# Softmax division moved from the probabilities to the gate of an attention block, by way of a row through DRAM

## Chip, core and metric

The program runs on one core of one Trainium2 chip. The metric is the device time of one execution in microseconds; the kernel before took 1666.42 us, the median of three runs between 1665.95 and 1667.75 us. Engines are named as in the profile: PE (matmuls), PEld (its weight loads), DVE, ACT, POOL, and SP, which only issues DMAs.

## What is computed

The reference is one layer: one input projection, two groups of mixers beside each other (sparse attention and a state-space scan), gates, one output projection and a LayerNorm. The attention's core, for each query block of 128 rows:

```python
s = jnp.einsum('bqgrd,bqkgd->bqgrk', qg, kg).astype(jnp.float32) * scale
s = jnp.where(valid[:, :, None, None, :], s, -jnp.inf)
p = jax.nn.softmax(s, axis=-1).astype(vg.dtype)
o = jnp.einsum('bqgrk,bqkgd->bqgrd', p, vg)
...
o_attn = _dsa_attention(q, k, v, q_idx, k_idx, w_idx) * jax.nn.silu(z_attn)
```

There are 1024 rows of 2048 columns, 8 query heads in 2 groups (4 heads share a key head), head width 128, and each query keeps 256 keys. The selection is a mask that is added to the scores, so the kernel works with whole rows of keys.

## The kernel before

Rows are handled in two halves of 512 (h = 0, 1). PE works through one long stream of matmuls: projection pieces (names `pj`, with x and w each split in a rounded high part `xh`, `wh` and a rest `xl`, `wl`, three matmuls for one product), and at the end the output projection, whose seven block products need what the mixers wrote to the DRAM tensors `mx` (`mx1_0` to `mx1_7` are the attention of the second half: two heads of a pair are two of these tensors). Weights come by DMA into `wr`, ACT rounds them to `wh`, DVE or POOL forms `wl`.

Everything else is written as Python generators (`t_attn`, `t_split`, `t_ssd` and more) that run beside the stream. A planner (`Flow`) steps a generator when its inputs, buffers and engines are free by the planner's own clock, and a second pass (`Queue.order`) puts the recorded calls in the order in which each engine gets them. Each engine then takes its instructions strictly in that order, and waits where an input is late. So a change to one task moves the order of nearly all that follows. For elementwise work that DVE or POOL may do, `Flow.pick` (L671) chooses by the same clocks.

The attention of one half and one key head (`t_attn`, L1852) is eight blocks: query blocks i, each as two pairs of heads pr. Three lanes take the blocks in turn. For one block:

- queries are loaded and split, PE makes the scores of the two heads in PSUM tiles `a`, `t_rowmax` (L1950) adds the mask, scales and takes the row maximum into the tile `pt`, which has (i+1)*128 columns;
- ACT takes the exponential in place and sums each row into `sm` (L1899), DVE the reciprocal of the two sums (L1901);
- POOL multiplies both `pt` tiles in place by their reciprocal (L1904, `gscale` L752);
- for each of the i+1 key blocks PE transposes a 128x128 piece of each head, `t_split` (L1958) rounds it on ACT and forms the rest on DVE, and PE multiplies by v into the PSUM tile `o`, where rows are the head's columns and columns are the queries (L1929 to L1931);
- DVE multiplies `o` by the gate (L1938), which was loaded as [128, 2, 128] from `z`, and two DMAs write the result to `mx` (L1943).

Of the kernel before, what the change touches and what calls it, by code (L numbers as in the profile page):

```python
# [13 lines left out]
ALU = mybir.AluOpType  # L14
# [4 lines left out]
P = 128  # L19
# [749 lines left out]
class Layer:  # L769
# [669 lines left out]
    def start_tasks(self):  # L1439
        fl = self.fl  # L1440
        fl.add(self.t_tables(0), 1, "rot", ROTS)
        self.ev_k = [Event(), Event()]
        self.ev_w = [Event(), Event()]
        self.ev_dt = [Event(), Event()]
        self.ev_row = [Event(), Event()]
        self.kk, self.score, self.nlog = {}, {}, [0, 0]
        self.ev_score = [Event(), Event()]
        self.ev_mask = {i: Event() for i in range(8)}
        self.m_sc = {i: self.scratch(f"mask{i}", [P, (i + 1) * P], BF) for i in range(2, 8)}
        self.ev_mask[0].cells = self.ev_mask[1].cells = [[0.0]]  # L1450
        self.mixed = [[self.scratch(f"mx{h}_{e}", [P, HALF]) for e in range(16)] for h in range(2)]
        self.hst = [self.scratch(f"hst{g}", [P, 256]) for g in range(4)]
        self.arow = [self.scratch(f"arow{h}", [64, P]) for h in range(2)]
        self.q_sc = [[self.scratch(f"q{h}_{g}", [4, P, HALF]) for g in range(2)] for h in range(2)]
        self.z_sc = [[self.scratch(f"z{h}_{g}", [4, P, HALF]) for g in range(2)] for h in range(2)]
        self.k_sc = [[self.scratch(f"k{h}_{g}", [P, HALF]) for g in range(2)] for h in range(2)]
        self.v_sc = [[self.scratch(f"v{h}_{g}", [P, HALF]) for g in range(2)] for h in range(2)]
        self.h_sc = [[[self.scratch(f"h{h}{s}_{d}", [P, HALF]) for d in range(4)] for s in range(4)] for h in range(2)]
        self.y_sc = {m: [self.scratch(f"y{m}_{k}", [P, HALF]) for k in range(8)] for m in (7, 6)}
        self.ev_y = {m: [Event() for _ in range(8)] for m in (7, 6)}  # L1460
        self.halves, self.left = [], {}
        self.ev_join = {(c, st): Event() for c in range(2) for st in range(4)}
        self.sums, self.ev_sum = {}, {(m, c, st): Event() for m in OUT for c in range(2) for st in range(4)}
        self.ev_kv = {(h, g, x): Event() for h in range(2) for g in range(2) for x in "kv"}
        self.ev_q = {(h, n): Event() for h in range(2) for n in range(8)}
        self.ev_z = {(h, n): Event() for h in range(2) for n in range(8)}
        self.ev_mix = {}
        for h in range(2):
            for e in range(16):
                self.ev_mix[h, e] = [Event() for _ in range(2 if e >= 8 else 4)]  # L1470
        self.ssd_n, self.ev_part = {}, {}
        self.p_sc = [[[self.scratch(f"pt{h}_{g}_{j}", [P, 2, HALF]) for j in range(3)] for g in range(4)] for h in range(2)]
        self.x_sc = {m: [self.scratch(f"x{m}_{k}", [P, HALF]) for k in range(8)] for m in (1, 2, 3, 4)}
        self.ev_x = {m: [Event() for _ in range(8)] for m in (1, 2, 3, 4)}
        self.stash, self.stt, self.prod, self.taken, self.backs = {}, {}, {}, set(), {}
        self.ev_h = {(h, g): Event() for h in range(2) for g in range(4)}
        self.tab = {}
        self.lnev = [Event() for _ in range(8)]
        self.ev_gain = Event()
        self.ev_rows = [Event() for _ in range(4)]  # L1480
        self.ev_res = {(prod, h, dc + c): Event() for prod, (h, dc) in self.ROWS.items() for c in range(2)}
        for k in range(8):
            src = [self.a["xt"][h, 8 * kh + k] for kh in range(2) for h in range(2)]
            fl.add(self.t_forms(src, {m: self.x_sc[m][k] for m in self.x_sc}, {m: self.ev_x[m][k] for m in self.x_sc}), 3, f"form_{k}", 100e3)
        self.o_sc = {m: [[self.scratch(f"o{m}_{c}_{k}", [P, 512]) for k in range(8)] for c in range(2)] for m in (1, 2, 3, 4)}
        for c in range(2):
            for k in range(8):
                src = [self.wo_at(n, c, k) for n in (11, 12, 21, 22)]
                fl.add(self.t_wforms(src, {m: self.o_sc[m][c][k] for m in self.o_sc}), 6, f"wform_{c}{k}", WFORMS + (8 * c + k) * WSTEP)
        for i in range(8):  # L1490
            fl.add(self.t_bias(i), 6, f"bias{i}", BIAS + i * WSTEP)
        for h in range(2):
            for blocks in ((2,), (3,)) if h == 0 else ((4, 7), (5, 6)):
                fl.add(self.t_topk(h, blocks), 3, f"topk{h}")
            for g in range(2):
                self.start_attention(h, g)
# [355 lines left out]
    def t_attn(self, h, g, st, todo):  # L1852
        fl, nc = self.fl, self.nc
        while todo:
            i, pr = todo.pop(0)
            n = (i + 1) * P
# [6 lines left out]
            pt = [fl.new("s4" if h else "u", [P, 1024 if h else 512]) for _ in heads]  # L1863
# [13 lines left out]
            sm = fl.new("sm", [P, 16])  # L1877
# [21 lines left out]
                fl.act(pt[r][:, 0:n], pt[r][:, 0:n], AF.Exp, bias=sm[:, 4 + r:5 + r], accum_out=sm[:, 6 + r:7 + r])  # L1899
            yield Need("V")  # L1900
            nc.vector.reciprocal(sm[:, 8:10], sm[:, 6:8])  # L1901
            yield Need("G")
            for r in range(2):
                fl.gscale(pt[r][:, 0:n], pt[r][:, 0:n], sm[:, 8 + r:9 + r])  # L1904
            fl.free(sm)
            yield Need("P", o=1, u=2)
            o = fl.new("o", [P, 256])
            gate = fl.new("u", [P, 2, P])
            fl.dma(gate, src(self.z_sc))
            spare = [fl.new("u", [P, 512], R)]  # L1910
            nk = i + 1
            ahead, kb = [], 0
            while kb < nk or ahead:
# [19 lines left out]
                if len(spare) > 1 and (len(spare) + len(ahead) > 3 or kb == nk):  # L1933
                    fl.free(spare.pop())
            fl.free(*spare, *pt)
            yield Need("V")
            g2 = gate.rearrange("p r s -> p (r s)")
            fl.tt("V", g2, o, g2, ALU.mult)  # L1938
# [2 lines left out]
            for r in range(2):  # L1941
                e = 4 * g + heads[r]
                fl.dma(self.mixed[h][e][:, q0:q0 + P], gate[:, r])  # L1943
                fl.signal(self.ev_mix[h, e][i - 4 * h])
            fl.free(gate)
            st["lanes"] += 1
            if st["lanes"] == 8:
                fl.signal(self.ev_att(h, g))
# [456 lines left out]
```

## Time and profile before

| what | value |
|---|---|
| median of three runs | 1666.42 us (1665.95 to 1667.75) |
| the profiled execution | 1665.7 us, span of its instructions 1663.9 us |
| PE busy | 1604.7 us, 96% of the span |
| DVE, ACT, POOL busy | 1345.0, 987.3, 271.9 us |
| DMA | 431.67 MB, mean 259 GB/s |

Busy time is a union of spans whose ends are modelled for PE: a matmul of 512 columns shows as about 0.39 us, but the next starts 0.227 us later. The granted clock is 1.00 from 52 us up to the last stretch. The work of the attention lies in four stretches, by its scaling instructions on POOL: 244 to 314 us, 756 to 861 us, 926 to 1045 us and 1134 to 1276 us.

### The profile page before, as it was taken

The page shows a single profiled execution, that of the slowest core. Times are in us where ns is not written, and L with a number is a line of the kernel's source. Part 1 is how long each engine was busy: PE and PEld are TensorE (multiplying, and loading weights), DVE is VectorE, ACT ScalarE, POOL GpSimd, SP SyncE. Part 2 cuts the span into 40 slices and gives each one's busy share as a digit, 9 for nine tenths or more (in the row PEclk, how much of TensorE's full clock was granted, in tenths as well). Part 3 has the DMA queues.
Part 4 walks back from the last instruction along what each step waited for, and adds up shares of the span by engine and source line. Part 5 has one row for each costly group of instructions (what it writes and reads, how often), then busy time and mean ns, then how long its engine had stood idle before and what let it go on. Part 6 is the DMA issues. An engine that isn't in the chain of part 4 may idle for free.

```text
span 1663.9 us, 26382 instructions
## 1 busy us (share of the span) xinstructions
PE 1604.7 (96%) x7989; PEld 1339.3 (80%) x7989; DVE 1345.0 (81%) x2991; ACT 987.3 (59%) x1920; POOL 271.9 (16%) x321
## 2 busy tenths in 40 slices
PE   7999999999999999999999999999999899999993
PEld 6888888888887888787788888888888788888782
DVE  7887655568899988898965777899986888988966
ACT  6657867565575599998832455657655444333431
POOL 3200022111114100101320322113111001000212
PEclk8999999999999999999999999999999999999997
DMA  9579998695477799999989886996766998878997
GB/s 311 167 243 366 299 254 233 205 315 153 133 206 232 226 303 300 302 276 296 334 272 340 266 280 195 290 297 208 229 206 191 301 337 260 270 238 297 336 231 177
DMA packets 272686, 431.67 MB, mean 259 GB/s; under 512 B 29600, under 2 KB 87328, under 8 KB 272032
## 3 DMA queue, kind: packets, MB, share of 16 engines
q1 hardware_dynamic: 259872, 406.93, 74.0%
q0 software_dynamic: 12672, 23.07, 9.3%
q8 instruction: 62, 1.02, 0.3%
q14 instruction: 80, 0.66, 0.1%
HBM read 338.56 MB, written 131.17 MB: 282 GB/s over the span
## 4 chain that ended last, share of the span: by engine, by line
PE 83%; DVE 8%; DMA 3%; issue 3%; ACT 1%; POOL 1%; SPq 0%; POOLq 0%; DVEq 0%; ACTq 0%
PE pj L467 64%; PE a L467 11%; PE o L467 8%; DVE u L467 3%; DMA wr<-wt 2%; DVE wl L467 1%; DVE wr L467 1%; DVE xl L467 1%; ACT u L467 1%; DVE s L467 1%; DMA u<-xn 1%; DVE sm L467 1%; ACT wh L467 0%; DMA u<-xt 0%; DMA u<-mx 0%
## 5 line engine op out<-in xcount | busy, mean ns | idle before, releaser
L467 PE MATMUL pj<-xh,wh 128*128 128x512 f32 (+1 forms) x1520 | 591.0, 389 | 7.5 <-ACT wh L467 4.2
L467 PE MATMUL pj<-xh,wl 128*128 128x512 f32 (+1 forms) x1520 | 582.6, 384 | 7.1 <-DVE wl L467 7.1
L467 PE MATMUL pj<-xl,wh 128*128 128x512 f32 (+1 forms) x1520 | 581.8, 383 | 0.2
L467 ACT ACTIVATE wh<-wr 128x512 fp32r<-128x512 f32 (+1 forms) x488 | 304.0, 626 | 400.3 <-PE pj L467 201.2
L467 DVE TENSOR_TENSOR wl<-wr,wh 128x512 fp32r<-128x512 f32 (+1 forms) x456 | 316.8, 700 | 117.1 <-ACT wh L467 112.7
L467 PEld LDWEIGHTS pj<-xh,wl 128*128 128x128 f32 x1520 | 287.5, 189 | 64.5 <-DVE wl L467 9.4
L467 PEld LDWEIGHTS pj<-xh,wh 128*128 128x128 f32 x1520 | 287.6, 189 | 60.6 <-ACT wh L467 5.6
L467 PEld LDWEIGHTS pj<-xl,wh 128*128 128x128 f32 x1520 | 287.7, 189 | 49.8 <-POOL xl L467 0.3
L467 PE MATMUL a<-u,u 128*128 128x512 f32 (+3 forms) x776 | 176.6, 344 | 3.3 <-DVE u L467 1.6
L467 DVE TENSOR_TENSOR u<-u,u 128x512 f32<-128x512 f32 (+7 forms) x240 | 150.6, 636 | 9.6 <-ACT u L467 7.7
L467 PEld LDWEIGHTS a<-u,u 128*128 128x128 f32 x776 | 129.8, 189 | 28.8 <-DVE s L467 5.4
L467 ACT ACTIVATE u<-u 128x512 f32<-128x512 f32 (+4 forms) x209 | 118.5, 576 | 55.7 <-DVE u L467 46.3
L467 ACT ACTIVATE u<-s,sm 128x1024 bf16<-128x1024 f32 (+7 forms) x132 | 128.8, 977 | 8.3 <-DVE sm L467 4.9
L467 PE MATMUL pj<-wh,xh 128*128 128x512 f32 x310 | 125.4, 404 | 2.5 <-DVE u L467 1.5
L467 PE MATMUL pj<-wh,xl 128*128 128x512 f32 x310 | 121.1, 392 | 1.5 <-DVE xl L467 1.5
L467 PE MATMUL pj<-wl,xh 128*128 128x512 f32 x310 | 120.9, 390 | 0.0
L467 ACT ACTIVATE xh<-u 128x512 fp32r<-128x512 f32 (+1 forms) x184 | 102.1, 585 | 29.5 <-DVE u L467 16.1
L467 DVE TENSOR_TENSOR wr<-wr,wr 128x512 f32<-128x512 f32 x160 | 115.4, 725 | 3.1 <-DMA wr<-wt 2.8
L467 DVE TENSOR_TENSOR xl<-u,xh 128x512 fp32r<-128x512 f32 (+1 forms) x168 | 113.0, 697 | 4.4 <-ACT xh L467 3.8
L467 ACT ACTIVATE a<-a 128x512 f32<-128x512 f32 (+3 forms) x160 | 77.2, 504 | 44.2 <-PE a L467 42.0
L467 POOL DMA_DIRECT2D o<-wo x64 | 53.8, 865 | 292.8 <-DMA o<-wo 137.3
L467 ACT ACTIVATE u<-a 128x256 fp32r<-128x256 f32 (+3 forms) x182 | 61.5, 363 | 63.8 <-PE a L467 58.8
(164 smaller groups left out, 2076.8 us busy)
## 6 DMA issues: line engine op xcount, KB each, us to landing
wr<-wt SPq DMA_DIRECT2D x424, 256.0 KB, 4.6
u<-xt SPq DMA_DIRECT2D x80, 256.0 KB, 5.5
u<-mx SPq DMA_DIRECT2D x72, 256.0 KB, 4.9
o<-wo POOLq DMA_DIRECT2D x64, 256.0 KB, 6.7
u<-x SPq DMA_DIRECT2D x64, 256.0 KB, 5.2
wr<-o SPq DMA_DIRECT2D x64, 256.0 KB, 4.6
pt<-u SPq DMA_DIRECT2D x48, 256.0 KB, 4.0
u<-pt SPq DMA_DIRECT2D x48, 256.0 KB, 4.5
```

The costliest lines, as they stand in the source:

```text
L467: f(*[self.place(x) for x in c.args], **{k: self.place(x) for k, x in c.kw.items()})
```

## The change

POOL's two multiplications of a block are gone: `pt` keeps the exponentials, of which the largest in a row is 1. The reciprocals (128 rows by 2 heads) are written from `sm` to a new DRAM tensor `r_sc`, in the program `rs<group>_<i>_<pr>`, and are read back with all 256 numbers in each of the 128 partitions, since in the tile `o` queries lie along the columns. The gate and this row share one buffer of 512 columns (`both`), so the block holds no more buffers than before. After the matmuls of the block the gate is multiplied by the row in place, on DVE or POOL as `pick` decides, and then, as before, by `o`.

```diff
@@ -1450,6 +1450,7 @@
         self.hst = [self.scratch(f"hst{g}", [P, 256]) for g in range(4)]
+        self.r_sc = {(g, i, pr): self.scratch(f"rs{g}_{i}_{pr}", [P, 2]) for g in range(2) for i in range(8) for pr in range(2)}
         self.arow = [self.scratch(f"arow{h}", [64, P]) for h in range(2)]
@@ -1899,14 +1900,16 @@
             yield Need("V")
             nc.vector.reciprocal(sm[:, 8:10], sm[:, 6:8])
-            yield Need("G")
-            for r in range(2):
-                fl.gscale(pt[r][:, 0:n], pt[r][:, 0:n], sm[:, 8 + r:9 + r])
+            r_sc = self.r_sc[g, i, pr]
+            fl.dma(r_sc, sm[:, 8:10])
             fl.free(sm)
             yield Need("P", o=1, u=2)
             o = fl.new("o", [P, 256])
-            gate = fl.new("u", [P, 2, P])
+            both = fl.new("u", [P, 2, 256])
+            gate, rows = both[:, 0].rearrange("p (r s) -> p r s", r=2), both[:, 1]
             fl.dma(gate, src(self.z_sc))
+            fl.dma(rows, r_sc.rearrange("s r -> (s r)").partition_broadcast(P))
+            here = Event(fl.last)
             spare = [fl.new("u", [P, 512], R)]
@@ -1933,6 +1936,8 @@
             fl.free(*spare, *pt)
+            yield Need("VG", ev=(here,))
+            fl.two(gate, gate, rows.rearrange("p (s r) -> p r s", r=2), ALU.mult)
             yield Need("V")
             g2 = gate.rearrange("p r s -> p (r s)")
             fl.tt("V", g2, o, g2, ALU.mult)
@@ -1942,7 +1947,7 @@
-            fl.free(gate)
+            fl.free(both)
```

The order of the instructions changes on every engine from the first attention block on. PE has the same 7,686 matmuls and transposes in both programs; the first 1,194 and the last 626 stand in the same order. In the whole program POOL loses 64 scalings; of the 32 new products 22 stand on DVE and 10 on POOL; SP gets 64 more issues.

One place matters for the prediction: the end of the last attention block (i = 7, pr = 1, which writes `mx1_6` and `mx1_7`), where the output projection has begun and needs `mx1_6`. PE before, from the block's last matmul (into `o_3053`) to the first matmul on `mx1_6` (`xh_3085`); `xh_3066` and `xh_3071` are `mx1_4` and `mx1_5`, and the rows of `a` and `o_3075` are a scan task:

```order
L467 MATMUL o_3053_14758<-u_3057_14756,u_2517_12676 128x256
L467 MATMUL a_3074_14811<-u_2822_13601,u_3004_14461 128x128 x2
L467 MATMUL o_3075_14832<-u_2826_13631,u_2824_13772 64x128 x2
...
L467 MATMUL pj_3014_14522<-wh_3024_14576,xh_3066_14857 128x512
...
L467 MATMUL o_3019_14549<-wh_3033_14609,xl_3072_14872 128x512
L467 MATMUL a_3111_14913<-o256_121,u_3076_14736 128x1 x2
...
L467 MATMUL a_3123_14954<-c3_158,u_3090_14640 128x128
L467 MATMUL pj_3014_14522<-wh_3045_14660,xh_3085_14960 128x512
```

PE now, the same stretch (the block's tile is `o_3059`, `mx1_5` is `xh_3049`, `mx1_6` is `xh_3091`):

```order
L467 MATMUL o_3037_14708<-wh_3053_14766,xl_3050_14822 128x512
L467 MATMUL o_3059_14840<-u_3063_14830,u_2510_12658 128x256 x2
L467 MATMUL o_3059_14840<-u_3063_14830,u_2511_12680 128x256
L467 MATMUL a_3081_14928<-u_2873_13776,u_2524_12429 128x128 x2
L467 MATMUL o_3082_14940<-u_2877_13887,u_2875_14079 64x128 x2
...
L467 MATMUL a_3117_14996<-c3_158,u_3085_14827 128x128
L467 MATMUL a_3116_15009<-c3_158,sm_3113_14993 128x128 x2
L467 MATMUL pj_3029_14669<-wh_3057_14782,xh_3091_15042 128x512
```

The 24 matmuls on `mx1_4` and `mx1_5`, which stood behind the block's last matmul, now stand ahead of it; between it and the first matmul on `mx1_6` are 22 small ones instead of 49 of which 24 are of 512 columns. From the block's last score matmul to its last matmul into `o` there are now 60 stream matmuls of 512 columns, 24 block matmuls of 256, 2 others of 256 and 16 transposes; before it was 33, 48, 2, and 32 with 2 others, since the other pair of this query block ended in the same stretch.

SP before, from the writes of that block's result to the reads:

```order
L467 DMA mx1_6_13447<-u_3054_14581 128x128
L467 DMA mx1_7_13452<-u_3054_14581 128x128
L467 DMA u_3082_14843<-arow0_1224 128x512
L467 DMA u_3083_14847<-arow0_1224 128x512
L467 DMA u_3095_14849<-arow1_4649 128x512
L467 DMA u_3104_14852<-mx0_0_3102 128x512
L467 DMA u_3120_14855<-mx1_2_10818 128x512
L467 DMA u_3107_14869<-mx1_1_10759 128x512
L467 DMA u_3108_14878<-mx0_1_3107 128x512
L467 DMA u_3087_14884<-mx1_6_13447 128x512
```

SP now, from the write of the reciprocals on:

```order
L467 DMA rs1_7_1_14787<-sm_3033_14700 128x2
L467 DMA wr_3069_14800<-o3_0_0_939 128x512
L467 DMA u_3085_14827<-pt0_3_1_12427 128x2x256
L467 DMA u_3097_14852<-hst2_14763 128x256
L467 DMA wr_3073_14861<-o3_0_1_2184 128x512
L467 DMA u_3060_14637<-rs1_7_1_14787 128x256
...
L467 DMA mx1_6_13575<-u_3060_14637 128x128
L467 DMA mx1_7_13590<-u_3060_14637 128x128
...
L467 DMA wr_3118_14976<-o3_0_3_3218 128x512
L467 DMA u_3121_14978<-mx1_2_11040 128x512
L467 DMA u_3093_14991<-mx1_6_13575 128x512
```

The row comes back five places behind its write; the read of `mx1_6` stands nine places behind its write, before it was nine as well.

## Rows read from the trace of the kernel before

**Rows 1.** The page: span, busy time by engine, chain that ended last.

```profile
span 1663.9 us, 26382 instructions
...
PE 1604.7 (96%) x7989; PEld 1339.3 (80%) x7989; DVE 1345.0 (81%) x2991; ACT 987.3 (59%) x1920; POOL 271.9 (16%) x321
...
PE 83%; DVE 8%; DMA 3%; issue 3%; ACT 1%; POOL 1%; SPq 0%; POOLq 0%; DVEq 0%; ACTq 0%
```

**Rows 2.** Windows: stretch, length, busy (count) PE, PEld, DVE, ACT, POOL; clock, DMA, GB/s.

```profile
208.00:1508.00 1300.00, 1281.89 (x6410) 1067.62 (x6409) 1065.62 (x2337) 793.86 (x1517) 212.82 (x242) 1.00 0.83 256
700.00:870.00 170.00, 162.36 (x768) 133.33 (x767) 147.53 (x357) 130.60 (x264) 36.36 (x34) 1.00 0.93 292
...
1248.00:1352.00 104.00, 97.89 (x528) 81.30 (x527) 80.48 (x174) 50.21 (x96) 6.67 (x6) 1.00 0.83 269
```

**Rows 3.** Groups on POOL: count, busy us, mean ns, idle before and its releasers.

```profile
L467 POOL TENSOR_SCALAR s<-s,sm 128x640 f32<-128x640 f32 (+3 forms) x32 | 36.5, 1160 | 121.9 <-DVE sm L467 91.7 <-ACT u L467 28.7 <-ACT wh L467 1.6
L467 POOL TENSOR_SCALAR u<-u,sm 128x128 f32<-128x128 f32 (+3 forms) x32 | 26.5, 837 | 76.0 <-DVE sm L467 42.9 <-issue 17.4 <-PE a L467 6.6
```

**Rows 4.** Groups by form on POOL: the like of the new product.

```profile
L467 POOL TENSOR_TENSOR u<-u 128x256 f32<-128x256 f32 x1 | 0.9, 892 | 0.9 <-ACT u L467 0.9
```

**Rows 5.** Groups by form on DVE: the like products, and wl.

```profile
L467 DVE TENSOR_TENSOR wl<-wr,wh 128x512 fp32r<-128x512 f32 x452 | 315.2, 703 | 112.6 <-ACT wh L467 108.2 <-PE a L467 1.0 <-DMA u<-x 0.4
...
L467 DVE TENSOR_TENSOR u<-u 128x256 f32<-128x256 f32 x15 | 6.3, 417 | 1.2 <-ACT u L467 1.0
...
L467 DVE TENSOR_TENSOR u<-u,s 128x512 f32<-128x512 f32 x4 | 2.7, 676 | 0.0
```

**Rows 6.** Groups by form on PE: transposes of a block among others.

```profile
L467 PE MATMUL a<-c,u 128*128 128x128 f32 x200 | 34.4, 275 | 3.8 <-POOL u L467 1.1 <-ACT u L467 1.0 <-PE a L467 0.9
```

**Rows 7.** Waits, all engines: us, times, longest.

```profile
PE pj L467 <- DVE wl L467: 7.1, 4, 4.6
```

**Rows 8.** Waits of SP: us, times, longest.

```profile
SPq L467 <- DVE wl L467: 217.1, 197, 4.9
```

**Rows 9.** Timeline of POOL, 801 to 832 us: start, length, what.

```profile
803.47 3.70 POOL L467 TENSOR_SCALAR u<-u,sm 128x256 f32<-128x256 f32 x2 [5.15 <-DMA u<-x]
```

**Rows 10.** DMA issues: KB each, median us from issue to landing.

```profile
u<-z SPq DMA_DIRECT2D x32, 128.0 KB, 4.5
mx<-u SPq DMA_DIRECT2D x64, 64.0 KB, 3.8
u<-arow SPq DMA_DIRECT2D x64, 64.0 KB, 3.9
```

**Rows 11.** The tile arow, a row read into all partitions: landing times.

```profile
DMA to landing us min/median/max: 1.8/4.5/8.7
```

**Rows 12.** Timeline of DVE, 243.5 to 258 us.

```profile
246.06 0.16 DVE L467 RECIPROCAL sm<-sm 128x2 f32<-128x2 f32 x1
...
252.27 0.42 DVE L467 TENSOR_TENSOR u<-o,u 128x256 f32<-128x256 f32 x1
```

**Rows 13.** Timeline of PE, 1263 to 1304 us.

```profile
1268.17 0.59 PE L467 MATMUL pj<-wh,xh 128*128 128x512 f32 x1
...
1287.36 0.61 PE L467 MATMUL a<-u,u 128*128 128x128 f32 x4
...
1303.53 0.50 PE L467 MATMUL pj<-wh,xh 128*128 128x512 f32 x1 [1.09 <-ACT xh L467]
```

**Rows 14.** Timeline of SP, 1276 to 1306 us.

```profile
1288.65 0.90 SPq L467 DMA_DIRECT2D mx<-u  x2
...
1291.68 6.53 SPq L467 DMA_DIRECT2D u<-mx  x7
```

**Rows 15.** The chain in order of time: start, length, what.

```profile
134.06 106.12 PE pj L467 x468
...
833.48 4.54 DMA wr<-wt
...
1296.53 6.29 DMA u<-mx
```

## Prediction

> **What bounds the kernel.** I read the page first, then the windows, the groups by line and by form, the waits, and last the timeline and the chain at the places where PE is idle. PE is busy 1604.7 of 1663.9 us, and 83% of the chain that ended last is PE [rows 1]. The change takes nothing from PE: the same matmuls are there before and now. It can only move PE's idle time, which is 1663.9 - 1604.7 = 59.2 us. Of that, 1300 - 1281.89 = 18.1 us lie between 208 and 1508 us [rows 2]; the other 41.1 lie at the start and in the tail, where the order is the same in both programs, so they stay. Two places make up most of the 18.1: 170 - 162.36 = 7.6 us between 700 and 870 us, where the DMA engines are busy 93% of the time, and 104 - 97.89 = 6.1 us between 1248 and 1352 us, where the output projection begins and waits for the last attention block [rows 2]. So the most that could be won is about 18 us, 1.1%, and a realistic part of it is a third or less.
>
> **What goes: 64 scalings on POOL.** They are 36.5 + 26.5 = 63.0 us of POOL's busy time [rows 3]. POOL has 212.82 us of work in 1300 [rows 2] and sets nothing by itself. What PE waited for them directly is 1.1 us, the transposes of a block released by POOL [rows 6]. I count -1.1 us. The scalings also disturb DVE, with which they overlap: two of 256 columns took 3.70 us at 803 us [rows 9], where the mean of one in this group is 0.84 [rows 3]. For DVE I bound it by its most frequent instruction: the rest of the weights `wl` takes 703 ns in the mean, the quickest like it 676, so all disturbance by anything costs it at most 452 x 27 ns = 12.2 us [rows 5]. The scalings are 63.0 / 212.82 = 30% of what POOL did there, which makes 3.7 us of DVE time.
>
> **What comes on DVE and POOL: 32 products.** 22 on DVE at 417 ns [rows 5] are 9.2 us, 10 on POOL at 892 ns [rows 4] are 8.9 us. So DVE is busy 9.2 - 3.7 = 5.5 us more, in 1300 us of which it works 1065.62 [rows 2]; its idle fifth hides that. If that cover is gone, the price is paid where PE waits for `wl`: all such waits together are 7.1 us, 4.6 of them one at the start [rows 7]. Between -1 us (30% of the other 2.5 are won) and +1 us (the same is lost) I take 0.
>
> **What comes on SP and the DMA engines.** 64 more issues at 0.90 / 2 = 0.45 us [rows 14] are 29 us of SP. SP waits 217.1 us for weight buffers to come free alone [rows 8], so the issues fit in; behind a write that waits for a late reciprocal stand weight loads, which run ahead of their use by several pieces. The bytes are 32 x 129 KB = 4.2 MB, 1% of the total. They cost something only where the DMA engines are full: eight blocks lie between 756 and 861 us, 8 x 0.131 = 1.05 MB, at 292 GB/s [rows 2] 3.6 us if every byte delayed a weight. The chain does run through weight loads there, one of 4.54 us at 833 us [rows 15], but in pieces. Between 0 and +3.6 I take +1 us.
>
> **The new wait.** The product of gate and row needs the write to land and the read to land. Nearest rows: a write of 64 KB to `mx` lands after 3.8 us, the gate's own load of 128 KB after 4.5, a row read into many partitions after 3.9 [rows 10], and over all such rows after 1.8 to 8.7 [rows 11]. So the way there and back is 0.45 + 3.8 + 0.45 + 4.5 = 9.2 us. It begins at the reciprocal, where the scalings were; the shortest time from a reciprocal to the product with `o` was 252.27 - 246.06 = 6.2 us [rows 12], in the blocks of one key block, while in the last block a pair needs about 14. In those short blocks the row is 3 us late, but nobody needs them soon, and DVE has other work ahead of the product. I take 0 here, and keep the case where this is wrong as a rival.
>
> The Trainium skill, page "DMA: Bandwidth & Descriptors", section "Specifications", says that transfers in pieces under 512 bytes are read, changed and written back. The new write is in pieces of 8 bytes, and no row here shows one so small; by that rule its landing would be later than the 3.8 us of the nearest row, and the sum would go toward the slower rival below.
>
> **The last attention block.** This is the largest term. Before, the last score matmul of the block is issued before 1268.17, its last matmul into `o` before 1287.36, and the first matmul on `mx1_6` starts at 1303.53 [rows 13]: 19.2 and 16.2 us. A stream matmul takes 106.12 / 468 = 0.227 us [rows 15]; I take those of 256 columns, transposes and other small ones at half of it. Before, the first stretch holds 33 x 0.227 + 84 x 0.113 = 17.0 us of PE work and the second 24 x 0.227 + 25 x 0.113 = 8.3, so PE lacks work for 2.2 + 7.9 = 10.1 us. Now the first stretch holds 60 x 0.227 + 42 x 0.113 = 18.4 us. The block itself needs 19.2 us less two scalings, which at 1160 ns [rows 3] are 2.3, thus 16.9; PE has enough to do, idle 0. The second stretch now holds 22 x 0.113 = 2.5 us, since the 24 matmuls on `mx1_4` and `mx1_5` went ahead. The way from the last matmul through the write and read of `mx1_6` is as before, with as many places on SP between them. It took 16.2 us; if SP had issued the read as soon as the write (1288.65 plus 0.45) had landed, 3.8 later, this would have been at 1292.9 and not at 1296.53 [rows 14, 15], and the way 12.6. So PE lacks work for 10.1 to 13.7 us now, against 10.1: between 0 and +3.6. I take +2. A row that comes later than `o` here would add to it; the way of 9.2 us begins at about the first transposes and the block's matmuls take from there some 10 us, so it is close.
>
> **The sum.** -1.1 + 0 + 1 + 0 + 2 = +1.9 us. Against the profiled execution's 1665.7 us this is 1667.6; the median of the runs is 0.7 above that execution, so I predict 1668.3 us, 0.1% over 1666.42. A measurement of this kernel can tell a change of about 0.2%, 3.3 us; by that this is no change.
>
> **Rivals.**
>
> *The new order closes idle time (faster).* The lanes no longer wait for POOL, so blocks end earlier, and the planner has new places for everything between 240 us and the tail. If half of the 7.6 + 6.1 us of the two places goes, with the 1.1, and the terms of +1 and +2 don't come, that is -8 us; a third makes -5.7. I give the case 1660.7 us. For it: 63 us of POOL work stood in the blocks' own chains. Against it: PE waited for POOL only 1.1 us, and at the last block the order shows no more work behind it.
>
> *The row is late (slower).* DVE takes its instructions in order, and 22 of the products stand on it ahead of `wl` and the splits of other blocks. Place: the blocks at 756 to 861 us, where the DMA is full and landings run long, and at 1134 to 1276. If both landings take 8.7 [rows 11] the way is 18.3 us, longer than a block of few key blocks. It decides once the row lands after the block's last matmul by more than the one or two instructions that DVE still has. Price: 16 blocks with 0.5 us passed on to PE are 8 us, 1676 with the sum, 1672 with half. For it: PE already waits in both stretches. Against it: the order puts 15 to 49 DVE instructions between a reciprocal and its product.
>
> *The last block alone (slower, smaller).* The way keeps its 16.2 us and full DMA engines cost all of 3.6: -1.1 + 3.6 + 3.6 = +6.1, 1672.5 us. It counts with the slower case.
>
> **Chances.** No change within 0.2%: 0.37, at 1668.3, own range 1663.1 to 1669.7. Faster: 0.29. Slower, the late row and the last block together: 0.34. The range for 8 in 10 takes in the faster rival's 1660.7 and half of the late row with some of the last block: 1660.5 to 1676.
>
> **What would show it.** No scalings on POOL and its busy time down by about 54 us; PE busy as before; DVE up by 5 us. A gap on PE of some 10 to 13 us in pieces ahead of the first matmul on the last `mx` pair shows the last term; a smaller one speaks for the faster rival. Waits of DVE on the DMA of the new row, above 5 us in total, or PE waits on `wl` in 756 to 861 us that were not there, show the late row. The prediction is wrong if idle time between 208 and 1508 us differs from 18 by more than 5 us.

## The result: 1706.9 us, 2.4% slower

The changed kernel takes 1706.91 us (median of four runs, 1706.09 to 1708.82) against 1667.09 for the kernel before in the same session; the ratio is 1.0242, 95% interval 1.0229 to 1.0255. The forecast of 1668.3 and its range up to 1676 are both missed, by 38.6 and 30.9 us.

### The profile after

The page of the changed kernel, as [rows 1]:

```profile
span 1704.8 us, 26438 instructions
...
PE 1618.8 (95%) x7989; PEld 1348.0 (79%) x7989; DVE 1344.6 (79%) x3015; ACT 988.9 (58%) x1922; POOL 212.0 (12%) x265
...
PE 74%; DMA 10%; DVE 7%; ACT 3%; issue 3%; SPq 1%; POOL 1%; POOLq 0%; DVEq 0%; ACTq 0%
```

The span is 40.9 us longer, in two parts. PE's idle time went from 59.2 to 1704.8 - 1618.8 = 86.0 us, +26.8. And the same 7989 records on PE now take 1618.8 us in place of 1604.7, +14.1, which the forecast didn't allow for at all. In the chain that ended last PE gave up 9 points, and DMA went from 3% to 10%.

The windows, as [rows 2], and below them three stretches around one stop of PE (clock, DMA share and GB/s stand last):

```profile
208.00:1508.00 1300.00, 1254.45 (x6187) 1042.35 (x6185) 1032.38 (x2294) 781.56 (x1494) 149.47 (x183) 0.99 0.85 252
700.00:870.00 170.00, 158.38 (x719) 130.31 (x718) 142.93 (x344) 126.83 (x257) 15.17 (x15) 0.96 0.93 279
1248.00:1352.00 104.00, 94.83 (x507) 80.35 (x506) 78.77 (x186) 58.35 (x111) 5.59 (x6) 0.95 0.73 213
```

```profile
780.00:790.00 10.00, 9.98 (x49) 7.97 (x47) 4.49 (x11) 5.23 (x11) 0.00 (x0) 1.00 0.87 102
796.00:799.00 3.00, 3.00 (x11) 2.52 (x11) 1.39 (x4) 1.66 (x5) 0.00 (x0) 0.50 0.88 264
800.00:810.00 10.00, 10.00 (x46) 8.27 (x45) 9.14 (x25) 9.18 (x18) 0.00 (x0) 1.00 0.85 250
```

Idle time between 208 and 1508 us is 45.6 us, where it was 18.1. From 780 to 790 us the DMA engines are busy 87% of the time and yet move 102 GB/s, where [rows 2] has 292 for the whole stretch before. Three of the new writes (`rs`) were issued just ahead, at 775.5 and from 778.8 us. PE then stops, and in the stretch behind the stop the granted clock is 0.50, that is 1.2 GHz of 2.4. Below are a weight load from the chain that leads to the end of this stop, issued at 782.75 and landed 8.69 us later (the median of such loads in this run is 5.2), and the timeline of PE (start, length; in brackets the idle time ahead and its releaser):

```profile
782.75 8.69 DMA wr<-wt
```

```profile
789.37 0.39 PE L467 MATMUL pj<-xh,wh 128*128 128x512 f32 x1
789.60 0.39 PE L467 MATMUL pj<-xl,wh 128*128 128x512 f32 x1
795.41 0.98 PE L467 MATMUL o<-u,u 128*128 128x256 f32 x3 [5.43 <-ACT wh L467]
...
796.62 0.63 PE L467 MATMUL pj<-xh,wh 128*128 128x512 f32 x1
797.04 0.63 PE L467 MATMUL pj<-xl,wh 128*128 128x512 f32 x1
...
799.87 0.39 PE L467 MATMUL pj<-xl,wh 128*128 128x512 f32 x1
800.10 0.40 PE L467 MATMUL pj<-xh,wl 128*128 128x512 f32 x1
```

One matmul starts 0.23 us behind the other before the stop, 0.42 after it, and 0.23 again from 799.4 us. So this stop cost its own length and then some microseconds at half speed. The changed kernel has seven stretches at 0.50 between 52 us and its last stretch, the kernel before none. PE worked 27.0 us in these seven; by an estimate from the two start-to-start times (0.23 and 0.42 us), about half of that, 13 us, is lost to the clock. That is most of the 14.1.

The issues of DMA (KB each, median us to landing); the last line is the new write:

```profile
u<-z SPq DMA_DIRECT2D x32, 128.0 KB, 5.4
u<-rs SPq DMA_DIRECT2D x32, 128.0 KB, 5.5
mx<-u SPq DMA_DIRECT2D x64, 64.0 KB, 4.2
u<-arow SPq DMA_DIRECT2D x64, 64.0 KB, 4.7
...
rs<-sm SPq DMA_DIRECT2D x32, 1.0 KB, 6.8
```

The write of 1 KB lands later than the 64 KB to `mx`. The transfers that were there before land later as well (4.5, 3.8 and 3.9 in [rows 10]): something holds up all traffic, not only the new row. Waits of all engines, and of SP, as [rows 7, 8]:

```profile
POOL u L467 <- DMA u<-rs: 36.7, 4, 20.3
...
DVE u L467 <- DMA u<-rs: 17.9, 11, 7.7
...
PE pj L467 <- DVE wl L467: 13.7, 6, 4.7
PE pj L467 <- ACT wh L467: 12.2, 5, 5.7
```

```profile
SPq L467 <- DVE wl L467: 222.3, 178, 7.6
SPq L467 <- DMA rs<-sm: 32.6, 17, 3.9
```

There are three suspects at once: DVE and POOL wait for the row, SP waits for the landing of its write with weight loads behind it, and PE waits for weights (`wh`, `wl`), some of which come late from DMA. Which of them makes the 40 us can't be read from this trace alone.

### The profile page after: what moved, and what is told of

It is laid out like the page before. It is cut to its first block, busy times and chain, and to the rows that moved or that the text cites. A ratio compares the mean times of both kernels' runs of the same rounds, so it can differ in the third digit from the quotient of the medians.

```text
span 1704.8 us, 26438 instructions
## 1 busy us (share of the span) xinstructions
PE 1618.8 (95%) x7989; PEld 1348.0 (79%) x7989; DVE 1344.6 (79%) x3015; ACT 988.9 (58%) x1922; POOL 212.0 (12%) x265
## 3 DMA queue, kind: packets, MB, share of 16 engines
q1 hardware_dynamic: 269088, 411.16, 75.7%
## 4 chain that ended last, share of the span: by engine, by line
PE 74%; DMA 10%; DVE 7%; ACT 3%; issue 3%; SPq 1%; POOL 1%; POOLq 0%; DVEq 0%; ACTq 0%
PE pj L467 57%; PE a L467 10%; PE o L467 7%; DVE u L467 3%; DMA wr<-wt 3%; ACT u L467 2%; DMA u<-q 1%; DMA u<-rs 1%; DVE wl L467 1%; DVE s L467 1%; DVE wr L467 1%; SPq L467 1%; DVE xl L467 1%; ACT wh L467 1%; DMA mx<-u 1%
## 5 line engine op out<-in xcount | busy, mean ns | idle before, releaser
L467 PE MATMUL pj<-xh,wh 128*128 128x512 f32 (+1 forms) x1520 | 594.1, 391 | 14.1 <-ACT wh L467 12.2
L467 DVE TENSOR_TENSOR wl<-wr,wh 128x512 fp32r<-128x512 f32 (+1 forms) x458 | 312.8, 688 | 106.7 <-ACT wh L467 98.6
L467 DVE TENSOR_TENSOR u<-u,u 128x512 f32<-128x512 f32 (+8 forms) x236 | 147.1, 631 | 18.6 <-ACT u L467 15.5
L467 ACT ACTIVATE u<-s,sm 128x640 bf16<-128x640 int16 (+7 forms) x132 | 128.9, 977 | 8.0 <-DVE sm L467 7.8
L467 PE MATMUL o<-u,u 128*128 128x256 f32 (+1 forms) x688 | 96.1, 291 | 10.7 <-ACT wh L467 5.4
```

The source lines that it names most:

```text
L467: f(*[self.place(x) for x in c.args], **{k: self.place(x) for k, x in c.kw.items()})
```

## The experiments

All were timed beside the kernel before, whose median was 1667.0 to 1667.7 us each time. Idle is span less PE busy of the one profiled execution, whose time can differ from the median (no_use: 1701.5 against 1709.8 us). Order "new" is the changed kernel's, "old" that of the kernel before; "own" is a new plan of the kernel before.

| run | order | median us | ratio, 95% interval | PE busy | idle |
|---|---|---|---|---|---|
| changed kernel | new | 1706.9 | 1.0229 to 1.0255 | 1618.8 | 86.0 |
| order_only | new | 1682.1 | 1.0074 to 1.0105 | 1612.0 | 67.6 |
| no_write | new | 1683.2 | 1.0087 to 1.0122 | 1610.8 | 67.9 |
| const_row | new | 1709.3 | 1.0236 to 1.0267 | 1624.6 | 82.5 |
| no_use | new | 1709.8 | 1.0219 to 1.0272 | 1618.0 | 81.5 |
| write512 | new | 1688.2 | 1.0102 to 1.0149 | 1610.2 | 74.8 |
| write128 | new | 1687.9 | 1.0104 to 1.0149 | 1614.3 | 70.6 |
| scatter8 | new | 1684.3 | 1.0095 to 1.0125 | 1614.2 | 68.6 |
| dve_row | new | 1689.9 | 1.0121 to 1.0167 | 1612.6 | 71.6 |
| before_writes | old | 1680.4 | 1.0057 to 1.0096 | 1609.6 | 66.5 |
| before_scatter | old | 1665.5 | 0.9975 to 0.9997 | 1604.0 | 57.9 |
| before_pitch64 | old | 1667.6 | 0.9992 to 1.0010 | 1608.7 | 57.0 |
| before_pitch256 | old | 1666.5 | 0.9984 to 1.0003 | 1605.2 | 57.4 |
| replan_up | own | 1672.0 | 1.0020 to 1.0039 | 1611.1 | 58.8 |
| replan_down | own | 1693.3 | 1.0136 to 1.0167 | 1616.2 | 75.7 |
| old_order_none | old | 1666.2 | 0.9979 to 1.0005 | 1606.8 | 57.0 |
| old_order_row | old | 1704.2 | 1.0215 to 1.0249 | 1620.0 | 81.6 |
| old_order_late | old | 1722.9 | 1.0306 to 1.0351 | 1629.4 | 95.9 |
| old_order_pool | old | 1687.0 | 1.0087 to 1.0132 | 1617.6 | 71.1 |

### Which part of the change: order, write, read or wait

The edits stand in the loop that plays the recorded calls in their final order, so the order of the changed kernel stays as it is. The division is left out of the result in all four. The two DMAs of a block and the product's operand (one listing for all four, with the runs that have each line named behind it):

```diff
+        rows = {c.args[0].tensor.name for c in queue.calls if c.op == "dma_start" and c.args[1].tensor.name.startswith("rs")}
         for c in queue.order():
             queue.done(c)
+            if c.op == "dma_start" and c.args[0].tensor.name.startswith("rs"):   # order_only, no_write
+                continue
+            if c.op == "dma_start" and c.args[1].tensor.name.startswith("rs"):   # order_only
+                continue
+            if c.op == "dma_start" and c.args[1].tensor.name.startswith("rs"):   # no_write, const_row
+                nc.sync.dma_start(player.place(c.args[0]), a["lng"][0:256].partition_broadcast(P))
+                continue
+            if c.op == "tensor_tensor" and c.kw["in1"].tensor.name in rows and c.kw["in0"].tensor.name == c.kw["in1"].tensor.name:   # order_only, no_use
+                c.kw["in1"] = plan.ones[:, None, :].to_broadcast([P, 2, P])
             player.play(c)
```

**order_only**, neither write nor read, the product with constant ones. 

> The changed kernel's order, with the 32 writes of the reciprocals and the 32 reads of the row left out and the 32 products kept, which multiply the gate by a constant of ones (so the division by the row sum is left out). Theory order (the new order of all engines is itself the worse one): 1695 to 1707 us, idle of PE as in the changed kernel. Theory round trip (waits for the write and the row stop SP, DVE and POOL): 1665 to 1675 us. Both in part: 1680 to 1690.

**const_row**, the write stays and no instruction reads what it wrote; the row is read from constants. 

> The changed kernel with its order, but the row is read from a constant in DRAM instead of the written reciprocals (so the division is replaced by a product with a constant); the writes of the reciprocals stay and nobody waits for them. Theory round trip, in its form that SP waits for the landing of the write ahead of the read (32.6 us of SP): 1675 to 1690 us. Theory small write (the pieces of 8 bytes hold up other transfers) and theory order: 1700 to 1708.

**no_write**, the same without the write. 

> As const_row, but the writes of the reciprocals are not issued at all; the row is read from a constant in DRAM and the products wait for it. Theory small write: 1670 to 1685 us, well under const_row. Theory round trip by SP's wait: the same as const_row. Theory order: 1695 to 1707.

**no_use**, all 64 DMAs stay, and the products don't use the row, so neither DVE nor POOL waits for it. 

> The changed kernel with its order and all 64 DMAs, but the products multiply the gate by a constant of ones (the division is left out), so DVE and POOL do not wait for the row. Theory round trip in its form that DVE (17.9 us) and POOL (36.7 us) wait for the row: 1675 to 1690 us. SP's wait, small write and order: 1700 to 1708.

The four fall into two pairs. With the writes 1709.3 and 1709.8 us, without them 1683.2 and 1682.1, however the row is read, used or waited for. So the writes make 26 us (const_row less no_write), the order, with the scalings gone and the products in, 14.7 (order_only less the kernel before), together the whole loss. The waits of DVE and POOL for the row, 17.9 and 36.7 us above, cost nothing here: without them (no_use) it is no quicker. The wait of the read for the write costs nothing either, since const_row is without it and as slow. But const_row doesn't free SP of all its 32.6 us: later DMAs on SP still stand until an earlier write has landed.

```profile
SPq L467 <- DMA rs<-sm: 16.6, 11, 3.5
...
SPq L2409 <- DMA rs<-sm: 5.2, 3, 2.0
```

So the price of the writes can reach PE by way of slower traffic, of SP's standing still, or of both.

### What in the write costs

**before_writes** puts the writes alone into the kernel before, whose order and result stay:

```diff
+        n = 0
...
             player.play(c)
+            if c.op == "reciprocal" and c.args[0].ap[-1][1] == 2:
+                n += 1
+                nc.sync.dma_start(player.pools["dram"].tile([P, 2], F, name=f"rs{n}"), player.place(c.args[0]))
```

> The kernel before in its own order, with one more DMA after each attention reciprocal: the 128x2 reciprocals are written to DRAM in pieces of 8 bytes, 32 writes of 1 KB; nobody reads them and nothing waits for them, and the probabilities are divided as before. Theory A, the small writes hold up all DMA traffic while they run and so starve PE of weights and queries: +18 to +30 us, 1685 to 1697, and PE gaps of over 2 us with a release by weights in the attention stretches that the kernel before doesn't have. Theory B, what costs is the new order alone, or writes hurt only in it: within 4 us of the kernel before, 1664 to 1671.

Measured 1680.4, between the two theories: the writes cost in the old order too, +13 us, about half of what theory A gave. Its sign, stops released by weights, did not come: PE's one stop of over 2 us that the kernel before doesn't have was released by a scaling on POOL. POOL had stood 8.56 us for the landing of `o<-o`; in before_scatter, the run further down whose writes differ only in their addresses, the same wait is 4.40 us:

```profile
819.92 0.84 POOL L467 DMA_DIRECT2D o<-wo  x1 [8.56 <-DMA o<-o]
...
825.72 0.48 PE L467 MATMUL a<-c,u 128*128 128x128 f32 x1 [5.93 <-POOL u L467]
```

```profile
809.82 0.84 POOL L467 DMA_DIRECT2D o<-wo  x1 [4.40 <-DMA o<-o]
```

**write512** has const_row's writes replaced by 128 pieces of 512 bytes (`big`, a [128, 128] tensor, from constants).

> As const_row (order of the changed kernel, row read from constants in DRAM, nobody waits for the writes), but each of the 32 writes is 64 KB in 128 pieces of 512 bytes, taken from a constant tile: 64 times the bytes in as many pieces. The reciprocals themselves are left out, so the division is. Theory A, it is the size of the piece: 1682 to 1688, as no_write (1683.2). Theory C, any further write issued on SP at this place costs the same, by its pieces or its place in the queue: 1705 to 1712, as const_row (1709.3).

1688.2: 64 times the bytes, 21 us less than the small pieces. That is theory A, 0.2 us above its range. **write128** (pieces of 128 bytes, side by side) and **scatter8** (the 8-byte pieces, 512 bytes apart) ask what is wrong with a small piece:

```diff
...
+            if c.op == "dma_start" and c.args[0].tensor.name.startswith("rs"):
+                big = player.pools["dram"].tile([P, P], F, name="big" + c.args[0].tensor.name)
+                nc.sync.dma_start(big[:, 0:2], player.place(c.args[1]))   # scatter8
+                continue
...
```

> As const_row (order of the changed kernel, row read from constants, nobody waits for the writes; the division is left out of the result), but the 128 pieces of 8 bytes of each write land 512 bytes apart in DRAM, not side by side within 1 KB. Theory F, each small piece costs, wherever it goes: 1703 to 1713, as const_row (1709.3). Theory G, it is that all 128 pieces fall into the same 1 KB, where they must take turns: 1682 to 1690, as no_write (1683.2) and write512 (1688.2).

> As write512 (the division left out in the same way), with pieces of 128 bytes side by side, 16 KB in each write. Theory F, every piece under 512 bytes is read, changed and written back at the same price: 1703 to 1713. Theory G, pieces cost by how many fall together in 1 KB, here 8 in place of 128: 1682 to 1692.

1684.3 and 1687.9, theory G twice: a piece of 8 bytes by itself is cheap. **before_scatter** repeats it with order and result of the kernel before, as a test of SP's part in before_writes; its one difference from before_writes is a [128, 128] tensor of which columns 0 and 1 are written.

> As before_writes (order of the kernel before, division as before, 32 more writes of 128 pieces of 8 bytes that nobody reads), but the pieces land 512 bytes apart. Theory G, pieces side by side hold up the DMA: 1664 to 1671, the 13 us of before_writes are gone. Theory J, SP's wait for the reciprocals ahead of the write, with weight loads behind it, made those 13 us: 1677 to 1684.

1665.5. The 13 us are gone (if anything 0.1% is won, which wasn't followed up), so SP's wait for the reciprocals ahead of a write costs nothing. Its waits for the landing of the writes fall with the loss, from 14.2 us in before_writes to 1.5. The two kernels issue the same DMAs in the same order with the same packets (277,295) and bytes (431.71 MB); only addresses differ. Two-microsecond windows of both at the beginning of the second attention stretch, with writes at 755.29 and 763.01 us in before_writes:

```profile
755.30:757.30 2.00, 2.00 (x11) 1.59 (x10) 2.00 (x7) 2.00 (x7) 1.95 (x3) 1.00 1.01 329
757.30:759.30 2.00, 2.00 (x11) 1.61 (x10) 2.00 (x7) 1.61 (x5) 0.76 (x1) 1.00 0.78 191
759.30:761.30 2.00, 2.00 (x11) 1.65 (x10) 2.00 (x2) 2.00 (x4) 0.00 (x0) 1.00 1.14 97
761.30:763.30 2.00, 1.05 (x5) 0.56 (x3) 1.68 (x2) 2.00 (x8) 0.00 (x0) 1.00 0.91 178
763.30:765.30 2.00, 1.93 (x8) 1.25 (x9) 1.95 (x5) 0.02 (x1) 1.77 (x3) 1.00 0.89 220
765.30:767.30 2.00, 2.00 (x12) 1.63 (x11) 2.00 (x8) 0.75 (x2) 0.42 (x1) 1.00 0.47 46
```

and at 754.82, 759.09 and 766.88 us in before_scatter:

```profile
754.80:756.80 2.00, 1.89 (x10) 1.29 (x9) 2.00 (x7) 2.00 (x6) 2.00 (x3) 1.00 1.00 371
756.80:758.80 2.00, 2.00 (x11) 1.65 (x10) 2.00 (x7) 1.53 (x3) 0.50 (x1) 1.00 0.94 288
758.80:760.80 2.00, 2.00 (x11) 1.65 (x10) 2.00 (x2) 2.00 (x6) 1.32 (x2) 1.00 0.87 244
760.80:762.80 2.00, 0.76 (x4) 0.34 (x3) 1.73 (x3) 1.76 (x6) 1.77 (x2) 1.00 1.07 244
762.80:764.80 2.00, 2.00 (x10) 1.27 (x10) 2.00 (x5) 0.00 (x0) 0.00 (x0) 1.00 0.97 214
764.80:766.80 2.00, 2.00 (x11) 1.66 (x10) 2.00 (x8) 1.00 (x2) 0.68 (x2) 1.00 0.78 229
```

Some microseconds after each write with pieces side by side the rate falls, to 97 and 46 GB/s; at 759.3 us the engines count as fully busy while they move 97 GB/s, about a quarter of the 371 in the quickest window below. In the window of 46 they are busy 47% of the time only, since SP issued nothing from 765.8 to 768.5 us. With the pieces apart the rate stays at 214 or above here. This stretch is one of the clearer ones: over all 32 writes the mean rate from 4 to 8 us behind the issue is 160 GB/s in before_writes and 234 in before_scatter, and from 0 to 4 us it is the same in both (231 and 227). The landing of these writes in before_writes and in before_scatter:

```profile
DMA to landing us min/median/max: 2.8/6.5/9.7
```

```profile
DMA to landing us min/median/max: 1.4/3.4/6.7
```

**before_pitch64** and **before_pitch256** are before_scatter with [128, 16] and [128, 64] tensors, for the distance at which it ends.

> As before_scatter, with the 8-byte pieces 64 bytes apart (128 of them in 8 KB). If only pieces within the same few tens of bytes hold one another up: 1663 to 1670, as before_scatter (1665.5). If it is pieces within the same 512 bytes or so, here 8 in place of 64: between, 1668 to 1674. If any close packing does it: 1677 to 1684, as before_writes (1680.4).

> As before_scatter, with the 8-byte pieces 256 bytes apart (128 of them in 32 KB). If pieces hold one another up only when several share 64 bytes, or share 512 bytes in numbers: 1663 to 1670. If two in the same 512 bytes are enough: 1672 to 1684.

1667.6 and 1666.5, no change from the kernel before: 64 bytes between the starts of two pieces are enough. What hurts lies closer; side by side, 8 pieces share 64 bytes, 16 times in each write. Distances between 8 and 64 bytes were not tried, so whether it is the shared 64 bytes isn't shown.

### Is the new order worse, or any new order?

**replan_up** and **replan_down** are the kernel before with its planner's price of a POOL instruction (`t = 230 + 0.88 * n`) at 240 and at 220.

> The kernel before with one number of the planner changed: its price of a POOL instruction 240 ns in place of 230. The computation is the same, and the order changes from the second quarter on. Theory D, the order of the kernel before is an unusually good one and any new plan loses as order_only did (+15 us): 1675 to 1685. Theory E, the order of the changed kernel loses by something of its own: 1663 to 1671.

> The kernel before with the planner's price of a POOL instruction 220 ns in place of 230; the computation is the same. Theory D (any new plan loses): 1675 to 1685. Theory E (the changed kernel's order has its own fault): 1663 to 1671.

1672.0 and 1693.3. The first lies between the two expectations, the second beyond what theory D gave. Two plans that differ from the kernel before by a number with no meaning lose 4.5 and 25.8 us; order_only's 14.7 lie between them. In replan_up idle time is as before (58.8 us), and the loss is on PE's busy time; its timeline:

```profile
816.92 0.38 PE L467 MATMUL a<-c,u 128*128 128x128 f32 x2
820.22 0.80 PE L467 MATMUL pj<-xh,wl 128*128 128x512 f32 x1 [2.92 <-DVE wl L467]
...
821.24 0.63 PE L467 MATMUL pj<-xl,wh 128*128 128x512 f32 x1
821.66 0.63 PE L467 MATMUL pj<-xh,wl 128*128 128x512 f32 x1
```

One stop of 2.9 us, and behind it the start-to-start time of 0.42 again. PE works 6.2 us at the half clock there, so about 3 of the 6.4 us that PE's busy time grew are the clock's (an estimate); the rest was not followed up. Not every stop does this: another of 3.02 us at 862.1 us in the same run has the clock at 1.00 behind it. So, on three draws, the order of the kernel before is a good one, and the changed kernel's an ordinary one. What in each order makes a stop was not followed up.

### What the change is worth without either

**old_order_none** is the kernel before whose playing loop skips POOL's 64 scalings and puts nothing in their place (the division is left out of the result).

> The kernel before without POOL's 64 scalings and with nothing in their place (the division is left out of the result): what the change can win at most. Prediction's step, PE waited for them only 1.1 us: 1663 to 1667. If DVE and the blocks gain more from it: 1650 to 1660. If other places drift, as every shift so far did: 1668 to 1676.

0.9992, with 1 in the interval: no gain is shown, and at most 0.2% is possible. The mean of `wl` on DVE is 704 ns, before it was 703 [rows 5], so the 3.7 us that the prediction took off DVE's work did not come there.

**dve_row** has the whole change in its own order, but DVE turns the reciprocals first, and the row is written in 8 pieces of 128 bytes:

```diff
+                nc.vector.reciprocal(pad[k][:, 0:2], player.place(c.args[1]))
+                nc.vector.transpose(turned[k], pad[k])   # 128x32, in blocks of 32x32
...
+                for r in range(2):
+                    nc.sync.dma_start(row[r].rearrange("(b s) -> b s", b=4), turned[k][r::32])
```

> The changed kernel in its own order with the whole computation, but the reciprocals reach DRAM in 8 pieces of 128 bytes in place of 128 of 8: DVE turns a 128x32 tile (the two columns of reciprocals and zeros) in blocks of 32x32, and two DMAs of 4 pieces write the rows; the read and the product are as in the changed kernel. If the cost is the number of small pieces: 1681 to 1688, what the order alone takes (1682.1). If waiting for a real row costs as well, which no run so far had together with quick writes: 1690 to 1700. If few pieces under 512 bytes are as bad as many: 1703 or more.

1689.9, between the first two expectations; runs spread from 1686.0 to 1694.1. 17 us of the 40 come back, the order's 15 stay, and up to 8 are for the real row, its 32 further issues and its waits together. So with quick writes the waits for the row may cost something that no_use, with slow ones, couldn't show.

**old_order_row** plays the same in the order of the kernel before: no scalings, the turned writes and the read right behind the reciprocal, and the product by the row on DVE just ahead of the one with `o`.

> The change within the order of the kernel before: no division on POOL, the reciprocals turned on DVE and written in 8 pieces of 128 bytes right after each reciprocal, read back into a buffer of its own, and DVE multiplies the gate by the row just ahead of the product with the scores' result; everything else stands where it stood. If the loss is the small pieces and the new order: 1663 to 1669, with 63 us of POOL work gone and about 16 us of DVE work added, both mostly off the path. If the row comes late for blocks in this order, DVE stands and PE with it: 1672 to 1685.

1704.2, beyond both expectations. SP's waits there (us, times, longest; L2419 is the read of the row):

```profile
SPq L2419 <- DMA rs<-turned: 86.2, 34, 5.6
```

Two runs ask whether that wait is the cause. **old_order_late** puts 3 SP places between reciprocal and writes and 8 between writes and read; **old_order_pool** issues the read on POOL's queue (`nc.gpsimd.dma_start`).

> As old_order_row, but the two writes of a block stand 3 SP places behind its reciprocal and the read of the row 8 places behind them (or just ahead of the product that uses it, if that comes first). Theory K, SP stood still for the landing of the writes, 86 us in all, with weight loads behind it: most of the 37 us go, 1664 to 1676. Theory L, the row is late for DVE in this order however it is issued: 1690 to 1706.

> As old_order_row, but the read of the row is issued from POOL's queue, so POOL waits for the landing of the writes and SP does not. Theory K: 1664 to 1680, SP's wait gone; what POOL does late (some weight rests and loads of its own queue) costs a part. Theory L: 1690 to 1706.

1722.9 and 1687.0: the one beyond theory L, the other between the two. Taking SP out of the wait gives 17 us back, so SP's wait is a part of it; but spacing on SP only moved the wait to DVE, and the time is longer; the waits of DVE (L2437, the product by the row), 10.2 us in old_order_row, are in old_order_late:

```profile
DVE u L2437 <- DMA row<-rs: 54.1, 11, 7.2
```

In this order, which was planned without the round trip, it loses 19 to 55 us wherever the wait was put. How these split between SP, DVE and POOL stays open. No version of the change is quicker than the kernel before, and old_order_none shows that in its order 0.2% is the most to be had.

## Why the prediction was wrong

**The step that failed** is the one on SP and the DMA engines: "The bytes are 32 x 129 KB = 4.2 MB, 1% of the total", priced from 0 to +3.6 us with +1 taken. It counted bytes and issues. The 32 KB of writes among them, the smallest transfers of the program, cost 25 us (const_row against scatter8), because their pieces of 8 bytes lay side by side in DRAM. The text took 3.8 us for their landing from a write of 64 KB, and the median is 6.8; it saw that no row had such small pieces, but bounded only that landing, as a delay for the product, and not what the write does to other traffic and to SP.

The Trainium skill's rule that the prediction set beside this (page "DMA: Bandwidth & Descriptors", section "Specifications": pieces under 512 bytes are read, changed and written back) pointed to the right side, and the late landing agrees with it, but alone it doesn't explain the cost. If it were the size of a piece that decides, scatter8, write128 and the two pitches would be as slow as const_row and before_writes; they aren't, and the landing (median 3.4 us in before_scatter against 6.5 in before_writes) isn't late. Whether pieces are read, changed and written back, and then wait for one another, no run here shows.

**The frame** failed too: "It can only move PE's idle time", 59.2 us of it, with "PE busy as before". PE has the same matmuls, but took 14.1 us longer for them, most of it at half the clock behind its stops. A stop that is added can cost more than its length, which the step on the last block left out as well. The signs for the other engines were nearer: POOL is 59.9 us less busy (54 said), DVE 0.4 less (5 more said).

**The order** was priced at that one block, +2 us of 0 to +3.6, with the rest of the new order as a rival that could only win (1660.7). The block itself came out near the forecast, in part by luck: PE's idle time from 1248 to 1352 us is 9.2 us against 6.1, +3.1 of 0 to +3.6, and the gaps sum to 9.1 where 10 to 13 were forecast. The text set that against 10.1 us of lacking work before, though [rows 2] has only 6.1 us of idle time there, so the text priced PE's matmuls there too low. The gaps:

```profile
1330.13 0.43 PE L467 MATMUL o<-u,u 128*64 128x128 f32 x2 [0.57 <-DVE u L467]
...
1334.99 0.77 PE L467 MATMUL a<-o,u 128*128 128x1 f32 x4 [3.95 <-DVE u L467]
1336.01 0.90 PE L467 MATMUL a<-c,u 128*128 128x128 f32 x3 [0.25 <-DVE sm L467]
...
1342.33 0.80 PE L467 MATMUL pj<-wh,xh 128*128 128x512 f32 x1 [4.32 <-ACT xh L467]
```

From 1335.3 to 1345.5 us, behind the first long gap and across the second, the granted clock is 0.50 and PE works 5.6 us, so by the same estimate the block lost some 3 us more. And the whole order costs 14.7 us; with neutral plans at +4.5 and +25.8 the forecast should have given it a wide range, mostly on the slow side.

**What held.** POOL's scalings: -1.1 us said, -1.5 measured (1666.2 against 1667.7), which the interval doesn't tell from no change. The products, as [rows 4, 5]:

```profile
L467 DVE TENSOR_TENSOR u<-u 128x256 f32<-128x256 f32 x37 | 16.5, 448 | 22.1 <-DMA u<-rs 17.9 <-DMA wr<-wt 4.2
```

```profile
L467 POOL TENSOR_TENSOR u<-u 128x256 f32<-128x256 f32 x11 | 9.3, 873 | 90.8 <-ACT u L467 45.1 <-DMA u<-rs 36.7 <-DMA rs<-sm 7.5
```

448 and 873 ns against the 417 and 892 taken, on engines with room. The new wait at 0 held beside the slow writes (no_use), and in this order it is worth at most the 8 us of dve_row; in the order before, the same round trip lost 19 us or more. The rival "the row is late" named the right symptom, waits of DVE above 5 us in all, but these 17.9 us cost nothing (no_use). The forecast's own sign of failure, idle time between 208 and 1508 us off by more than 5, came: 27.4.

## To carry to other kernels

Don't write a column that is spread over partitions into DRAM side by side: give each small piece 64 bytes of its own, or turn the column on chip first; and price a small write by what it does to all other traffic, not by its bytes. Count a stop of PE as its length and, where the granted clock falls, the slow stretch behind it. Where a planner sets the order, take every edit as a new draw: measure a few neutral plans first, and compare the edit within one fixed order.

## What had not been expected of the hardware

- 128 pieces of 8 bytes that are neighbours in DRAM slow the other DMA traffic some microseconds later (in the mean of 32 writes to 160 GB/s from 4 to 8 us behind the issue, where the same program with the pieces apart moves 234), and 32 such writes cost 13 us in one order and 25 in the other. At 64 bytes from start to start they cost nothing (1.0001, 0.9992 to 1.0010). That they wait for one another at the same 64 bytes is a reading; the trace shows no such queue. How the cost reaches PE, by slower loads, by SP or by POOL, was not separated.
- Behind stops of 2.9 and 5.4 us PE ran at the granted clock of 0.50 for some microseconds, while it had work; behind one of 3.02 us it stayed at 1.00.
